# Expert stages of a two-layer network: where the counts become integers, and where the one-hots of the fetched pairs are built

## The chip, the cores and the metric

One NeuronCore of one Trainium2 chip runs the whole program. The metric is the device time of one execution, in microseconds (us). Five engines work side by side: TensorE (PE; its weight loads are PEld), VectorE (DVE), ScalarE (ACT), GpSimd (POOL) and SyncE (SP), which issues the weight transfers.

## The reference, cut to what matters

A sequence of 256 tokens of width 1024 passes through two blocks of two layers. Each of the two layers of the first block ends in a mixture of experts, and the change is in that part alone:

```python
scores = sigmoid(t @ router_w); sel = scores + router_b
best_group = argmax(sum of the two best of sel in each of 4 groups)
top_idx = the two best experts of that group;  top_w = their scores / sum
for e in range(16):
    he = silu(t @ w_gate[e]) * (t @ w_up[e])          # 1024 -> 512
    y = y + combine[:, e:e+1] * (he @ w_down[e])      # 512 -> 1024
```

Each token goes to two experts of one group of four. The 16 experts' weights are 96 MiB in each layer, and all of them are read.

## The kernel before

`moe(l)` runs twice, once for each layer of the first block. The experts go in eight pairs, p = 0 to 7. Each pair has 64 places for each of its two experts; a token beyond them goes through conditional blocks. The stage goes in this order:

- Router: `logits`, `scored`, ranks on VectorE, then `pick` (chosen or not) and `rk` (each token's place in its expert), `cnt` (the larger count of each pair) and `cs` (the weights).
- `hot` and `gather` bring the tokens of pairs 0 and 1 (`FIRST = 2`) to their places: a product with a one-hot gives `ph` in PSUM, and ScalarE writes it, scaled, to `hg`. `gather(0, 4)` stands ahead of the first pair's products and `gather(4, 8)` in the middle of its gate product.
- `tokens_of` builds one-hots (`ohb`, 12 operations of VectorE, L1393) for pairs 2 to 7; `indices` turns them into token numbers (`px`, `number`, `idx`). By these numbers GpSimd fetches those pairs' rows from a copy in DRAM (`rows`).
- `up(p)`: 32 products for the gate (`pg`) and 32 for the up weights (`pu`), all at L1482, then `hd`, and its transpose `hidT`. `down(p)`: 32 products `po` (L1531), scaled (`of`), split in two (`eo`); the scatter back into `x` (`py`) is held over into the next pair.
- Weights come by SyncE's queue in transfers of 1 MiB, 12 for a pair, into a ring of 17 slots, in order of use; a slot is filled again when the products that read it are done.

For pairs 2 to 7 there are conditional blocks. Every engine that takes part has to load the count into a register:

```python
count = nc.values_load(cnti[0:1, p:p + 1], min_val=0, max_val=S, engines=engines)  # L1669
with tc.If(count > 64):                                                            # L1671
    Sm, ws = more_up(p, W, hidT)
own = up(p, W, (lambda: rest(p, p - 5)) if p in (5, 6) else None)
with tc.If(count > 64):                                                            # L1674
    more_down(W, hidT, Sm, ws)
```

`rest`, at p = 5 and 6, does the same with the largest count (L1616, block at L1618). `cnti` is made by one conversion (L1341) of all eight counts to integers.

The order of each engine's instructions is not that of the text: a planner picks it from a modelled timeline, from what is ready. `pin(...)` sets an instruction behind the one that stands before it in the text on the same engine. The products at L1482 and L1531 are pinned, and so are the products of `gather` and the differences `xl` (L1273); in the kernel before the one-hots `ohb`, the conversion and the register loads are not.

Of the kernel before, what the change touches and what calls it, by code (L numbers as in the profile page):

```python
# [14 lines left out]
I32 = mybir.dt.int32  # L15
AF = mybir.ActivationFunctionType
ALU = mybir.AluOpType
# [4 lines left out]
P = 128  # L22
D = 1024
S = 256
# [9 lines left out]
FIRST = 2  # L34
# [86 lines left out]
class Net:  # L121
# [1107 lines left out]
    def moe(self, l):  # L1229
        nc, I, tc = self.nc, self.I, self.tc  # L1230
        V = nc.vector
        mm = nc.tensor.matmul
        A, B = self.scale_shift(l, 1)
        with self.phase(f"moe{l}", MOE_RING, True) as mp:
# [3 lines left out]
            pin = tc.keep_in_program_order  # L1238
            rbias = self.rbias
            gate = self.gate[l, 5]  # L1240
            slots = self.k("slots")
# [93 lines left out]
            cnt = mp.tile([1, 8], F32, name="cnt")  # L1335
# [1 line left out]

            V.tensor_scalar(cnt[:, 0:FIRST], cnt[:, 0:FIRST], 32.0, None, op0=ALU.add)
            V.tensor_reduce(cnt[:, 0:1], cnt, axis=AX.X, op=ALU.max)
            cnti = mp.tile([1, 8], I32, name="cnti")  # L1340
            V.tensor_copy(cnti, cnt)  # L1341


            cs = mp.tile([P, 2, 16], F32, name="cs")
# [42 lines left out]
            def tokens_of():  # L1387
                for h in range(2):
                    for t in range(2):
                        o = self.sp.tile([P, 3, 256], BF16, tag=("e2", "gt")[h], name="ohb")  # L1390
                        e = rk[:, t, 4 + 6 * h:10 + 6 * h].rearrange("p (q j) -> p q j", j=2).unsqueeze(3)
                        for c, n, s0 in ((0, 64, 0), (128, 32, 64), (192, 32, 64)):
                            V.tensor_tensor(o[:, :, c:c + 2 * n].rearrange("p q (j s) -> p q j s", j=2),  # L1393
                                            e.to_broadcast([P, 3, 2, n]),
                                            slots[:, s0:s0 + n].unsqueeze(1).unsqueeze(1).to_broadcast([P, 3, 2, n]),
                                            op=ALU.is_equal)
                        ones_of.append(o)

            def indices():
# [67 lines left out]
            def up(p, W, between=None):  # L1467

                if p == 0:
                    oneh.extend(hot((0, 1), 0, 64))  # L1470
                    parts(1, True)
                    gather(0, 4)
                    tokens_of()
                q = slice(128 * (p % 2), 128 * (p % 2) + 128)
                pg = self.bank([P, 512], name="pg")
                pu = self.bank([P, 512], name="pu")
                for w, pp in ((W[0], pg), (W[1], pu)):
                    for k in range(KD):
                        if p == 0 and w is W[0] and k == 4:
                            gather(4, 8)  # L1480
                        for j in range(2):
                            pin(mm(pp[64 * j:64 * j + 64, :], hg[0][:, p % 2, k, 64 * j:64 * j + 64], w[j][k // 4][:, k % 4, :],  # L1482
                                   start=k == 0, stop=k == KD - 1, tile_position=(0, 64 * j)))
                if between:
                    between()
                if p == 0:
                    self.split(cs, ch, cl)
                    indices()
                hd = self.sp.tile([P, 512], F32, tag="e1", name="hd")
                nc.scalar.activation(hd, pg, AF.Silu)  # L1490
                V.tensor_tensor(hd, hd, pu, op=ALU.mult)  # L1491

                if self.pending:
                    self.pending(2)
                hidT = self.sp.tile([P, 4, P], F32, tag="e2", name="hidT")
                turn_hidden(hd, hidT)
                if self.pending:
                    self.pending(2)
                Sm, ws = places([oneh[t][:, q] for t in range(2)], p) if p < FIRST else own_places.pop(0)
                if 1 <= p < 7:  # L1500
                    columns(got[0][:, (p + 1) % 2, 0:D], P, hg[0][:, (p + 1) % 2])
                    own_places.append(known(p + 1, 0, kept[:, p % 2, :]))
                    if p < 6:
                        rows(1, p + 2)
                    if p < 5:
                        rows(0, p + 3)
                return hidT, Sm, ws
# [91 lines left out]
            engines = (mybir.EngineType.PE, mybir.EngineType.DVE, mybir.EngineType.Activation)  # L1599
# [13 lines left out]
            def rest(p, t):  # L1613


                left = nc.values_load(cnti[0:1, 0:1], min_val=0, max_val=2 * S,  # L1616
                                      engines=engines + (mybir.EngineType.Pool,))
                with tc.If(left > 96):  # L1618
                    wv = mp.tile([P, 16], F32, tag="wv", name="wv")
                    space = [e.rearrange("p a d -> p (a d)")[:, 0:2048] for e in got]  # L1620
                    hc = hg[0][:, (p + 1) % 2]
                    hid = self.sp.tile([P, 4, P], F32, tag="e1", name="hide")
                    banks = [self.bank([P, 512], name="be") for i in range(6)]
                    V.tensor_scalar(wv[:, 0:2 * FIRST], rk[:, t, 0:2 * FIRST], 64.0, None, op0=ALU.is_gt)
                    V.tensor_scalar(wv[:, 2 * FIRST:], rk[:, t, 2 * FIRST:], 96.0, None, op0=ALU.is_gt)
                    V.tensor_tensor(wv, wv, cs[:, t, :], op=ALU.mult)
                    nc.gpsimd.dma_start(space[0][:, 0:D], xd[128 * t:128 * t + 128, 0:D])
                    columns(space[0][:, 0:D], P, hc, banks[0:2])
                    n = 0

                    def fetched(src, nd):
                        nonlocal n
                        n += 1
                        return self.fetch(space[n % 2].rearrange("p (k n) -> p k n", n=nd), src, "(p k) n -> p k n", nc.gpsimd)
                    for e in range(NE):
                        for i, src in enumerate(("exp_w_gate", "exp_w_up")):
                            for b in range(2):
                                w = fetched(I[src][l, e][512 * b:512 * b + 512, :], 512)
                                for k in range(4):
                                    mm(banks[2 + i], hc[:, 4 * b + k, :], w[:, k, :], start=b + k == 0, stop=b + k == 4)  # L1640
                        hd = self.sp.tile([P, 512], F32, tag="gt", name="hde")
                        nc.scalar.activation(hd, banks[2], AF.Silu)
                        V.tensor_tensor(hd, hd, banks[3], op=ALU.mult)
                        turn_hidden(hd, hid, banks[0])
                        for b in range(2):
                            w = fetched(I["exp_w_down"][l, e][256 * b:256 * b + 256, :], D)
                            for k in range(2):
                                for c in range(2):
                                    mm(banks[4 + c], hid[:, 2 * b + k, :], w[:, k, 512 * c:512 * c + 512], start=b + k == 0,
                                       stop=b + k == 2)  # L1650
                        for c in range(2):
                            sl = slice(512 * c, 512 * c + 512)
                            of = self.sp.tile([P, 512], F32, tag="gt", name="ofe")
                            V.scalar_tensor_tensor(of, banks[4 + c], wv[:, e:e + 1], gate[:, sl], op0=ALU.mult, op1=ALU.mult)
                            V.tensor_tensor(self.x[:, t, sl], self.x[:, t, sl], of, op=ALU.add)
                    for i, q in ((0, p + 1), (1, p + 1), (0, p + 2)):
                        if q < 8:
                            rows(i, q)

            for p in range(8):  # L1660
                W = first_two(p) + [weights("exp_w_down", 256, p)]
                if p == 7:
                    self.turn, self.nload = [self.ring] * RING, 0
                    self.resume()
                if p < FIRST:
                    down(W, *up(p, W))
                    continue

                count = nc.values_load(cnti[0:1, p:p + 1], min_val=0, max_val=S, engines=engines)  # L1669
                hidT = self.sp.tile([P, 4, 64], F32, tag="e2", name="hidTb")  # L1670
                with tc.If(count > 64):  # L1671
                    Sm, ws = more_up(p, W, hidT)
# [3 lines that stand above are left out]
                down(W, *own, p == 7)  # L1676
# [789 lines left out]
```

## Time and profile before

| | |
|---|---|
| median of 3 runs | 1591.37 us (1589.22 to 1593.0) |
| profiled execution, its own time | 1589.33 us |
| span of its trace | 1587.5 us |
| TensorE busy | 1481.6 us, 93% of the span |
| VectorE busy | 916.3 us, 58% |
| ScalarE busy | 673.7 us, 42% |
| granted TensorE clock, mean | 0.979 of full speed |
| DMA | 418.14 MB, mean 263 GB/s |

The trace shows about 1.8 us less than the execution's own time, which lie around the span. Busy TensorE time is modelled for the ends of the matmuls, so start to start tells more than the durations. The first expert stage begins at about 200 us with its router and ends at about 451 us; the second begins at about 598 us and ends at about 846 us.

### The profile page before, as it was taken

What the parts mean: (1) busy time and instruction counts of PE and PEld (TensorE: products, weight loads), DVE (VectorE), ACT (ScalarE), POOL (GpSimd) and SP (SyncE); (2) the same over time, 40 slices, a digit from 0 to 9 for tenths busy, and PEclk for the clock granted to TensorE, in tenths of its full rate; (3) what the DMA queues carried; (4) which work ended last, traced back from release to release, by engine and by line L of the source; (5) the groups of instructions that cost most, each with busy time, mean ns of one, the idle gap of its engine ahead of it and who ended that gap; (6) DMA issues with size and microseconds to landing.
All of it is one profiled execution on the core that took longest, in us unless ns stands there. A gap on an engine that the chain in (4) does not pass through costs nothing. (4 is left out here: it accounts for less than half of the span.)

```text
span 1587.5 us, 22950 instructions
## 1 busy us (share of the span) xinstructions
PE 1481.6 (93%) x8719; PEld 1043.2 (66%) x8719; DVE 916.3 (58%) x1788; ACT 673.7 (42%) x1404; POOL 141.3 (9%) x192
## 2 busy tenths in 40 slices
PE   6999969998989997999888999899999999999998
PEld 3666634334369973444335887788887997788886
DVE  4755543233269974223226776866667777766665
ACT  3434331111146543111105455665556666665554
POOL 0320001000000000100002100110001211110000
PEclk9999989999989998999999999999999999999999
DMA  9998979999967986999997541646554542546540
GB/s 357 350 314 298 355 310 419 418 418 417 412 212 249 318 322 271 419 418 417 418 417 248 149 134 67 198 161 206 192 171 152 176 144 81 190 155 205 193 159 27
DMA packets 172511, 418.14 MB, mean 263 GB/s; under 512 B 10376, under 2 KB 94016, under 8 KB 147792
## 3 DMA queue, kind: packets, MB, share of 16 engines
q1 hardware_dynamic: 165696, 403.46, 68.7%
q0 software_dynamic: 6400, 12.78, 2.4%
q8 instruction: 89, 1.46, 0.4%
q14 instruction: 54, 0.44, 0.1%
q10 hardware_dynamic: 272, 0.00, 0.0%
HBM read 422.13 MB, written 3.19 MB: 268 GB/s over the span
## 5 line engine op out<-in xcount | busy, mean ns | idle before, releaser
L230 DVE TENSOR_TENSOR hl<-w,hl 128x1024 fp32r<-128x1024 f32 x280 | 336.4, 1234 | 52.9 <-ACT hl L229 52.8
L229 ACT CAST hl<-w 128x1024 fp32r<-128x1024 f32 x280 | 280.2, 1045 | 33.5 <-DMA w<-in_even_w_in 20.5
L2341 PE MATMUL pgu<-hT,hl 128*128 128x512 f32 x640 | 224.3, 394 | 0.0
L2342 PE MATMUL pgu<-hT,hl 128*128 128x256 f32 x640 | 177.1, 277 | 0.0
L381 PE MATMUL lin<-hl,hThi 128*128 128x256 f32 (+2 forms) x480 | 159.4, 335 | 1.4 <-ACT hl L229 0.8
L382 PE MATMUL lin<-hl,hThi 128*128 128x256 f32 (+2 forms) x480 | 153.9, 321 | 2.0 <-DVE hl L230 1.9
L383 PE MATMUL lin<-hl,hTlo 128*128 128x256 f32 (+2 forms) x480 | 152.8, 320 | 0.0
L1482 PE MATMUL pg<-w,hg 128*64 128x512 f32 x512 | 120.1, 616 | 20.7 <-issue 17.0
L2341 PEld LDWEIGHTS pgu<-hT,hl 128*128 128x128 f32 x640 | 119.9, 187 | 27.8
L1491 DVE TENSOR_TENSOR hd<-hd,pu 128x512 f32<-128x512 f32 x16 | 11.0, 688 | 196.9 <-PE pu L1482 196.9
L1482 PE MATMUL pu<-w,hg 128*64 128x512 f32 x512 | 116.4, 593 | 6.0 <-DMA w<-in_exp_w_up 4.9
L2342 PEld LDWEIGHTS pgu<-hT,hl 128*128 128x128 f32 x640 | 120.2, 188 | 2.0
L1531 PE MATMUL po<-w,hidT 128*64 128x512 f32 x512 | 114.4, 599 | 6.0 <-PEq L1674 3.1
L381 PEld LDWEIGHTS lin<-hl,hThi 128*128 128x128 f32 x480 | 92.9, 194 | 16.8 <-issue 8.1
L1482 PEld LDWEIGHTS pg<-w,hg 128*64 128x64 f32 x512 | 41.6, 141 | 94.6 <-issue 78.8
L382 PEld LDWEIGHTS lin<-hl,hThi 128*128 128x128 f32 x480 | 93.0, 194 | 11.2 <-DVE hl L230 3.8
L383 PEld LDWEIGHTS lin<-hl,hTlo 128*128 128x128 f32 x480 | 92.7, 193 | 7.0 <-DVE hl L230 0.8
L1482 PEld LDWEIGHTS pu<-w,hg 128*64 128x64 f32 x512 | 41.4, 137 | 77.4 <-issue 67.0
L1531 PEld LDWEIGHTS po<-w,hidT 128*64 128x64 f32 x512 | 37.5, 138 | 72.8 <-issue 63.8
L1546 ACT CAST eo<-of 128x512 fp32r<-128x512 f32 x32 | 19.8, 617 | 132.4 <-DVE of L1543 132.2
L381 PE MATMUL linc<-hThi,hl 128*128 128x256 f32 x224 | 66.2, 296 | 0.0
L1438 ACT ACTIVATE hg<-hgT,ab 128x128 f32<-128x128 f32 x48 | 18.1, 457 | 110.3 <-PE hgT L184 110.2
(571 smaller groups left out, 2856.2 us busy)
## 6 DMA issues: line engine op xcount, KB each, us to landing
w<-in_exp_w_gate SPq DMA_DIRECT2D x64, 1024.0 KB, 17.8
w<-in_exp_w_down SPq DMA_DIRECT2D x64, 1024.0 KB, 19.8
w<-in_exp_w_up SPq DMA_DIRECT2D x64, 1024.0 KB, 17.3
w<-in_ada_w SPq DMA_DIRECT2D x48, 1024.0 KB, 7.2
w<-in_ffn_wg SPq DMA_DIRECT2D x22, 1024.0 KB, 5.5
w<-in_ffn_wu SPq DMA_DIRECT2D x22, 1024.0 KB, 7.5
w<-in_ffn_wd SPq DMA_DIRECT2D x22, 1024.0 KB, 8.9
w<-in_even_w_in SPq DMA_DIRECT2D x14, 1024.0 KB, 10.5
```

Source lines behind the costliest of these rows:

```text
L229: pin(self.nc.scalar.copy(w[:, 0], src))
L230: pin(self.nc.vector.tensor_tensor(w[:, 1], src, w[:, 0].bitcast(F32), op=ALU.subtract))
L381: pin(mm(out, lh, rh, start=start, stop=False))
L382: pin(mm(out, lh, rl, start=False, stop=False))
L383: pin(mm(out, ll, rh, start=False, stop=stop))
L1438: nc.scalar.activation(out[:, k, :], pt[:, k, :], AF.Identity, scale=self.ab[:, 0, b, k:k + 1], bias=self.ab[:, 1, b, k:k + 1])
L1482: pin(mm(pp[64 * j:64 * j + 64, :], hg[0][:, p % 2, k, 64 * j:64 * j + 64], w[j][k // 4][:, k % 4, :], start=k == 0, stop=k == KD - 1, til ...
L1491: V.tensor_tensor(hd, hd, pu, op=ALU.mult)
L1531: pin(mm(po[c][64 * j:64 * j + 64, :], hidT[:, k, 64 * j:64 * j + 64], W[2][j][k // 2][:, k % 2, 512 * c:512 * c + 512], start=k == 0, sto ...
L1546: nc.scalar.copy(eh[c], of)
L2341: mm(pp[i], wh[:, k, :], both[:, :, k, :], start=k == 0, stop=False)
L2342: mm(pp[i][:, 0, :], wl[:, k, :], hi[:, k, :], start=False, stop=k == KD - 1)
```

## The change

Three edits, all in `moe`. The one conversion of all counts becomes seven of one element each, each into a tile of its own: the count of pair p + 1 is converted behind the products `pg` and `pu` of pair p (for p = 1 to 6), that of `rest` behind those of pair 3, each pinned on VectorE. The register loads read those tiles. `tokens_of` moves from ahead of the first pair's products to behind them and behind the split of `cs`, and its operations are pinned.

```diff
             V.tensor_scalar(cnt[:, 0:FIRST], cnt[:, 0:FIRST], 32.0, None, op0=ALU.add)
             V.tensor_reduce(cnt[:, 0:1], cnt, axis=AX.X, op=ALU.max)
-            cnti = mp.tile([1, 8], I32, name="cnti")
-            V.tensor_copy(cnti, cnt)
+            number_of = {}
+
+            def count_of(*who):
+
+                for i in who:
+                    number_of[i] = mp.tile([1, 1], I32, name=f"cnti{i}")
+                    pin(V.tensor_copy(number_of[i], cnt[:, i:i + 1]))
...
                         for c, n, s0 in ((0, 64, 0), (128, 32, 64), (192, 32, 64)):
-                            V.tensor_tensor(o[:, :, c:c + 2 * n].rearrange("p q (j s) -> p q j s", j=2),
...
+                            pin(V.tensor_tensor(o[:, :, c:c + 2 * n].rearrange("p q (j s) -> p q j s", j=2),
...
                     gather(0, 4)
-                    tokens_of()
...
+                if FIRST <= p + 1 < 8:
+                    count_of(p + 1)
+                if p == 3:
+                    count_of(0)
                 if between:
                     between()
                 if p == 0:
                     self.split(cs, ch, cl)
+                    tokens_of()
                     indices()
...
-                left = nc.values_load(cnti[0:1, 0:1], min_val=0, max_val=2 * S,
+                left = nc.values_load(number_of[0][0:1, 0:1], min_val=0, max_val=2 * S,
...
-                count = nc.values_load(cnti[0:1, p:p + 1], min_val=0, max_val=S, engines=engines)
+                count = nc.values_load(number_of[p][0:1, 0:1], min_val=0, max_val=S, engines=engines)
```

## Rows read from the trace of the kernel before

**Rows 1.** The page's chart: DMA busy in tenths, 40 slices of 39.7 us.

```profile
DMA  9998979999967986999997541646554542546540
```

**Rows 2.** Timeline of PE, first stage: start, duration, line, out<-in, count, idle before.

```profile
213.04 0.28 PE L1375 MATMUL ph<-kept,xl 128*128 128x256 f32 x1
222.55 5.72 PE L1482 MATMUL pg<-w,hg 128*64 128x512 f32 x16 [9.23 <-issue]
228.19 0.39 PE L1375 MATMUL ph<-kept,xh 128*128 128x256 f32 x1
...
230.28 3.65 PE L1482 MATMUL pg<-w,hg 128*64 128x512 f32 x16
233.77 7.04 PE L1482 MATMUL pu<-w,hg 128*64 128x512 f32 x32
240.74 0.75 PE L1405 MATMUL px<-tok,ohb 128*128 128x1 bf16 x24
```

**Rows 3.** Timeline of PE, second stage, at the same place.

```profile
612.23 0.38 PE L1375 MATMUL ph<-kept,xl 128*128 128x256 f32 x1
620.41 6.46 PE L1482 MATMUL pg<-w,hg 128*64 128x512 f32 x16 [7.79 <-issue]
626.80 0.39 PE L1375 MATMUL ph<-kept,xh 128*128 128x256 f32 x1
```

**Rows 4.** Tile cnti: line, engine, operation, duration ns min/median/max, first and last start.

```profile
L1669 PEldq TENSOR_LOAD <-cnti x12: 294/299/487, 216.8 to 619.6; - x12
...
L1616 PEldq TENSOR_LOAD <-cnti x4: 305/308/309, 219.7 to 618.9; - x4
...
L1341 DVE CAST cnti<-cnt x2: 152/152/153, 216.6 to 614.6; 1x8 int32<-1x8 f32 x2
```

**Rows 5.** Timeline of DVE, first stage.

```profile
210.44 2.01 DVE L1273 TENSOR_TENSOR xl<-xn,xh 128x512 fp32r<-128x512 f32 x2
212.38 2.82 DVE L1393 TENSOR_TENSOR ohb<-rk,kt 128x384 bf16<-128x384 f32 x8
...
215.20 0.17 DVE L1349 TENSOR_TENSOR cs<-cs,den 128x32 f32<-128x32 f32 x1
...
216.57 0.15 DVE L1341 CAST cnti<-cnt 1x8 int32<-1x8 f32 x1
```

**Rows 6.** Timeline of ACT, first stage.

```profile
215.40 0.22 ACT L203 CAST ch<-cs 128x32 fp32r<-128x32 f32 x1 [6.99 <-DVE cs L1349]
215.54 1.93 ACT L1379 ACTIVATE hg<-ph,ab 128x256 f32<-128x256 f32 x4
```

**Rows 7.** Windows of the first stage: busy by engine, PEclk, DMA share, GB/s.

```profile
218.00:220.00 2.00, 0.00 (x0) 0.00 (x0) 0.00 (x0) 0.00 (x0) 0.00 (x0) 0.50 0.90 371
220.00:222.00 2.00, 0.00 (x0) 0.00 (x0) 0.00 (x0) 0.00 (x0) 0.00 (x0) 0.50 0.21 88
...
228.00:230.00 2.00, 2.00 (x17) 1.81 (x16) 0.00 (x0) 0.56 (x2) 0.00 (x0) 1.00 0.40 74
```

**Rows 8.** Windows of the second stage.

```profile
614.00:616.00 2.00, 0.00 (x0) 0.00 (x0) 0.82 (x5) 1.48 (x4) 0.42 (x1) 0.97 0.67 277
```

**Rows 9.** Line L1618, the branch around `rest` on PE.

```profile
L1618 PEldq COMPARE_BRANCH  x4: 5888/5960/6163, 380.4 to 795.9; - x4
```

**Rows 10.** Timeline of PE around the first branch of `rest`.

```profile
377.81 7.07 PE L1482 MATMUL pu<-w,hg 128*64 128x512 f32 x32
386.69 0.48 PE L1518 MATMUL py<-eo,kept 128*128 128x512 f32 x1 [1.81 <-PEq L1618]
```

**Rows 11.** The page's costliest groups: busy, mean ns, idle before, its releaser.

```profile
L1482 PE MATMUL pu<-w,hg 128*64 128x512 f32 x512 | 116.4, 593 | 6.0 <-DMA w<-in_exp_w_up 4.9
```

**Rows 12.** Timeline of PE, second stage, pair 5: the first such wait.

```profile
759.38 3.65 PE L1482 MATMUL pu<-w,hg 128*64 128x512 f32 x16 [1.30 <-DMA w<-in_exp_w_up]
```

**Rows 13.** Timeline of DVE: the last operation of down(0), during pair 1's products.

```profile
252.19 0.69 DVE L1547 TENSOR_TENSOR eo<-of,eo 128x512 fp32r<-128x512 f32 x1 [0.68 <-ACT eo L1546]
```

**Rows 14.** Timeline of PE: pair 1's first products.

```profile
250.14 7.04 PE L1482 MATMUL pg<-w,hg 128*64 128x512 f32 x32
```

More of the change, by code (lines that the diff above doesn't have):

```diff
@@ L1392, in tokens_of @@
                         for c, n, s0 in ((0, 64, 0), (128, 32, 64), (192, 32, 64)):
-                            V.tensor_tensor(o[:, :, c:c + 2 * n].rearrange("p q (j s) -> p q j s", j=2),
-                                            e.to_broadcast([P, 3, 2, n]),
-                                            slots[:, s0:s0 + n].unsqueeze(1).unsqueeze(1).to_broadcast([P, 3, 2, n]),
-                                            op=ALU.is_equal)
+                            pin(V.tensor_tensor(o[:, :, c:c + 2 * n].rearrange("p q (j s) -> p q j s", j=2),
+                                                e.to_broadcast([P, 3, 2, n]),
+                                                slots[:, s0:s0 + n].unsqueeze(1).unsqueeze(1).to_broadcast([P, 3, 2, n]),
+                                                op=ALU.is_equal))
                         ones_of.append(o)
```

## The prediction

> **What bounds the kernel now.** I read the chart first. DMA is at nine tenths from the seventh to the eleventh and from the 17th to the 21st slice, the two expert stages, and lower just before each [rows 1]. That looks like a kernel bound by weights; the timeline of TensorE says otherwise. All waits of the `pu` products for up weights come to 4.9 us in 16 pairs [rows 11], and the first stands in pair 5 of the second stage [rows 12]. In the first stage TensorE works from its first pair to its last nearly without a stop, so the end of that stage is set by when TensorE begins, and by what stops it on the way.
>
> So the beginning is the place to look. In the first stage the last product of `gather(0, 4)` starts at 213.04 and ends at about 213.32, and the first gate product starts at 222.55, 9.23 us later, with no releaser named ("issue") [rows 2]. In the second stage the same gap is 7.79 us, from 612.61 to 620.41 [rows 3]. What ends it? The gate product needs `hg`. ScalarE writes its first four parts from 215.54 on, in 1.93 us [rows 6], so all are there at 217.5, and PE still does not start for 5 us. What fills these 5 us are register loads: PE's loads of all the counts, six at L1669 and two at L1616 in each stage, begin at 216.8 [rows 4], right when the conversion is done (216.57 + 0.15 = 216.72 [rows 5]), and eight of them until 222.55 make 5.8 / 8 = 0.72 us each, of which 0.3 is the load itself. The planner has put them ahead of the first pair. This is the stall the change can take away.
>
> [...] And DMA runs dry: all 17 slots are full, its share falls to 0.21 in the window from 220, and comes back in the one from 228 [rows 7], when the first slots are read out.
>
> **The change, part by part.** *Conversions.* Seven of one element take the place of one of eight: at 0.15 us each [rows 4] one more microsecond of VectorE in a stage, spread over pairs 1 to 6. There VectorE waits for PE for most of each pair's products, so I count nothing; without that cover it would be 0.9 us in a stage. The gain lies in the data they carry: no load can now come before its conversion, and the first conversion is pinned behind the last operation of `down(0)`, which runs from 252.19 [rows 13], in pair 1. All eight loads leave the gap.
>
> *One-hots.* Eight of the 12 operations stand on VectorE between `xl` (until 212.45) and the normalizing of `cs` at 215.20 [rows 5], and `ch`, which ScalarE does ahead of `hg`, waits for `cs` [rows 6]. Pinned behind the split of `cs`, they leave this chain: `cs` can run at 212.45, that is 2.75 us sooner, `ch` and `hg` with it. So `hg` begins at 215.54 - 2.75 = 212.8, and its first part is there at about 213.4 (1.93 / 4 = 0.48 apart, the first a little longer). The 12 one-hots take 12 x 2.82 / 8 = 4.2 us [rows 5] and would run from about 213 to 217. Who needs them? `px`, at 240.74 now [rows 2], some 229 then: 12 us of cover. Were it gone, `px` and the row fetches behind it on GpSimd's queue would be late next.
>
> *Queues.* The write of `cs` to DRAM (GpSimd) goes out 2.75 us sooner; the three first row fetches move with the products. SyncE's weight transfers keep their order and go out when slots come free, sooner by what PE gains.
>
> *What PE then does, first stage.* It starts at 213.4 instead of 222.55. The 16 products took 228.19 - 222.55 = 5.64 us to the next one's start, mostly at the lower clock; at the full clock the same 16 take 233.77 - 230.28 = 3.49 us [rows 2]. PE has then been idle for hardly 0.1 us, and the lower clock stood in the rows only deep in the long gap, so I take 3.49. The second half of the gather starts at 213.4 + 3.49 = 216.9, not 228.19: **11.3 us**. The first slots come free at 216.9, while DMA still has work (share 0.90 from 218 to 220 [rows 7]), so its gap closes, about 9 us (by the shares of these windows, 220.2 to 229.2). If the stage had no slack in its weights, DMA's 9 us would be the limit and not 11.3: that is the lower bound of this term, and I take the upper one, since PE hardly waits for weights in this stage.
>
> *Second stage.* The DVE and ACT rows repeat there, 2.0 us earlier against PE's first products (four `hg` parts from 613.55). Moved up by 2.75 they are early enough for PE to go on right behind the gather, at 612.61: 612.61 + 3.49 = 616.1 against 626.80 [rows 3]: **10.7 us**. DMA's share is 0.67 in the window from 614 [rows 8], so it runs dry about when the first slots come free, and its own gain is as long as PE's.
>
> Together 22.0 us a run, if the loads cost nothing where they go.
>
> *The loads' new places.* The trace of before does not show a load amid products. Bounds: nothing, or all of 0.72 us. For nothing speaks the branch around `rest`: on PE it takes 5.96 us from 380.4 [rows 9], and the idle time it leaves is 1.81 us [rows 10], because the products ahead of it ran on until 384.9. PE's sequencer is thus some 4.5 us ahead of the array, and a load of 0.72 us fits in. For the full price speaks that the load must wait for its conversion: if the planner puts it where the conversion has just ended, the sequencer stands there, the lead is used up, and the array waits 0.72 us. Between these ends I take half: 8 x 0.36 = 2.9 us in the first stage (0 to 5.8). In the second, lost time is made up at the waits for up weights, 4.9 us [rows 11], which are DMA's and not PE's: 0 to 0.9, I take 0.4.
>
> [...]
>
> Sum: 11.3 + 10.7 - 2.9 - 0.4 = 18.7 us. Against the profiled execution's 1589.33: 1570.6. That execution lies 2.0 us below the median of the runs (1591.37), so the median of the changed kernel should be 1572.7. Less than 0.2% (3 us) can't be told from no change here.
>
> **The rivals.** *Loads at full price and more* (faster, by less): each load also waits about half a microsecond for its conversion. Then 8 x 1.2 = 9.6 in the first stage and 9.6 - 4.9 = 4.7 in the second: 22.0 - 14.3 = 7.7 us, 1583.7. For it: the planner did put these loads as early as it could. Against: the lead of 4.5 us.
>
> *Something else ready takes the loads' place.* `px` depends on the one-hots alone and is not pinned; put ahead of the gate products it makes PE wait until 217.2, and 0.75 for itself, and the clock is down again. Per stage 4.5 + 2.2 us of the gain are lost: 22.0 - 13.4 - 3.3 = 5.3, 1586; with the loads at full price it is a change of less than 3 us. Against: in the kernel before `px` was ready by 217 too and stayed behind the products [rows 2].
>
> *Slower.* A load put at the head of a pair's products, for a conversion pinned on VectorE behind work that ends late. In pair 1 that work ends at 252.88 [rows 13], and the products start at 250.14 [rows 14]: with conversion and load PE would stand until 253.8, 3.6 us. Eight such are 29 us in the first stage and 29 - 4.9 = 24 in the second: 53 - 22 = 31 us slower, 1622. It decides from 1.4 us a load in the first stage (11.3 / 8) and 1.95 in the second (15.6 / 8). Against: a planner that goes by what is ready would issue products there.
>
> *The lower clock anyway.* [...] On the rows, 16 products at the lower clock cost 2.2 us more in the first stage and 2.9 in the second: 18.7 - 5.1 = 13.6 us, 1577.7.
>
> **How the numbers follow.** The forecast (loads from free to 0.72, full clock) 0.57; lower clock 0.10; loads at full price and more 0.15; another instruction in their place 0.10; slower 0.05; the rest, some 0.03, no gain for a reason I don't see. Faster takes the first three and most of the fourth: 0.88; same 0.07; slower 0.05. The range goes from all of 22.0 with 3 us of scatter (1566) to the loads' rival with 2 us (1586).
>
> **What would show it.** In the profile after: no register load of PE between `gather(0, 4)` and the first gate product, which starts within 1 us of the gather's end; `ohb` behind `cl` on VectorE; granted clock 1.00 through the first pair; no dry stretch of DMA at either stage's start; and some 11 us less from `gather(0, 4)` to `gather(4, 8)` in each stage. Wrong if the idle time comes back amid pairs 1 to 6 at L1482 or L1669, or if PE waits for weights in pairs 5 and 6 by more than the 4.9 us of now, or if the next part of the kernel has to wait for its own weights and gives the time back.

## The result, and the profile after

The changed kernel takes 1570.58 us (median of 4 runs, 1568.27 to 1572.58) against 1590.46 of the kernel before on the same chip: 19.9 us less, a ratio of 0.9873 with a 95% interval of 0.9853 to 0.9892. The span of the profiled execution went from 1587.5 to 1567.2 us, by 20.3. The forecast was 18.7 us and 1572.7.

Where it came from is seen in the timeline of TensorE in the changed kernel, first and second stage (columns: start, duration, engine, line, operation, count, idle time before):

```profile
210.56 0.41 PE L1380 MATMUL ph<-kept,xh 128*128 128x256 f32 x1
...
213.54 0.28 PE L1380 MATMUL ph<-kept,xl 128*128 128x256 f32 x1
214.19 3.65 PE L1486 MATMUL pg<-w,hg 128*64 128x512 f32 x16 [0.37 <-ACT hg L1384]
217.77 0.39 PE L1380 MATMUL ph<-kept,xh 128*128 128x256 f32 x1
...
219.87 3.65 PE L1486 MATMUL pg<-w,hg 128*64 128x512 f32 x16
223.35 7.04 PE L1486 MATMUL pu<-w,hg 128*64 128x512 f32 x32
...
246.59 7.04 PE L1486 MATMUL pu<-w,hg 128*64 128x512 f32 x32
253.56 0.51 PE L1527 MATMUL py<-eo,kept 128*128 128x512 f32 x1
...
257.74 7.09 PE L1540 MATMUL po<-w,hidT 128*64 128x512 f32 x32
...
601.88 0.37 PE L1380 MATMUL ph<-kept,xl 128*128 128x256 f32 x1
602.18 3.65 PE L1486 MATMUL pg<-w,hg 128*64 128x512 f32 x16
605.76 0.39 PE L1380 MATMUL ph<-kept,xh 128*128 128x256 f32 x1
```

The gap of 9.23 us ahead of the first product [rows 2] is 0.37 us long, and what ends it is `hg`, a cause the profile can name. In the second stage [rows 3] there is none. The 16 products take 217.77 - 214.19 = 3.58 us where they took 5.64. `pu` of the first pair starts at 223.35 instead of 233.77. The stage itself began 0.47 us later in this execution (first `ph` at 210.56 instead of 210.09), so the gain there is 10.9 us.

The granted clock (the column before DMA's share) is 1.00 through the first stage's start, and DMA's share does not fall (0.93 to 1.05 from 210 to 226); in the second stage the clock is at 0.50 in the window before the products start, and DMA has a short dip from 604 to 608 (shares of 0.52 and 0.59):

```profile
214.00:216.00 2.00, 1.81 (x10) 0.67 (x12) 2.00 (x8) 1.51 (x4) 0.14 (x1) 1.00 1.04 430
...
218.00:220.00 2.00, 2.00 (x18) 1.86 (x19) 0.09 (x1) 0.97 (x3) 0.00 (x0) 1.00 1.04 439
...
600.00:602.00 2.00, 2.00 (x11) 2.00 (x10) 1.72 (x8) 1.24 (x3) 0.75 (x1) 0.50 1.01 426
602.00:604.00 2.00, 2.00 (x12) 0.68 (x12) 2.00 (x7) 1.02 (x2) 0.00 (x0) 0.98 1.01 426
604.00:606.00 2.00, 2.00 (x12) 0.62 (x9) 0.74 (x3) 0.00 (x0) 0.00 (x0) 1.00 0.52 217
```

The rows of [rows 7] at the same place had 0.50 for the clock and 0.21 for DMA.

Now the loads. By tile, in the changed kernel (duration in ns min/median/max, first and last start):

```profile
L1346 DVE CAST cnti<-cnt x14: 131/142/143, 242.4 to 633.6; 1x1 int32<-1x1 f32 x14
...
L1678 PEldq TENSOR_LOAD <-cnti x12: 297/301/488, 250.0 to 643.5; - x12
...
L1625 PEldq TENSOR_LOAD <-cnti x4: 298/299/303, 253.0 to 642.8; - x4
```

They begin at 250.0, in pair 1, and the order of PE's instructions in that pair (read from the built program, not from the trace; the number is the place in PE's stream) puts six in a row between `py` and the transpose `hT`, two more ahead of `po`:

```
896 L1486 MATMUL pu<-w,hg 64x512 [waits DMAHW5_49,PE_49]
...
904 L1527 MATMUL py<-eo,kept 128x512 [waits PE_49]
905 L1528 MATMUL py<-eo,kept 128x512
906 L1678 TENSOR_LOAD cnti_2172 [waits DVE_49]
907 L1678 ISA x2
908 L1678 TENSOR_LOAD cnti_2402 [waits DVE_49]
...
916 L1678 TENSOR_LOAD cnti_3181 [waits DVE_49]
917 L1678 ISA x2
918 L184 MATMUL hT<-kt,hd 128x128 [waits DVE_49]
```

Eight loads are some 5.8 us of the sequencer; from `pu` to `po` of pair 1 PE takes 257.74 - 246.59 = 11.15 us, and before it took the same 11.15 without any load there (257.00 to 268.15). They are free. The six in a row take 6 x 0.72 = 4.3 us from 250.0 on, and PE works on without a pause, past the transpose `hT` at 254.60; of the other two, the last in the second stage starts at 643.5, and there too PE works without a pause until `po` starts at 645.73.

On VectorE the one-hots now stand behind `cl` and delay nobody, and all seven conversions, the first here, run in pair 1, not pair by pair:

```profile
212.93 0.17 DVE L1354 TENSOR_TENSOR cs<-cs,den 128x32 f32<-128x32 f32 x1
213.39 0.19 DVE L204 TENSOR_TENSOR cl<-cs,ch 128x32 fp32r<-128x32 f32 x1 [0.28 <-ACT ch L203]
213.50 4.11 DVE L1398 TENSOR_TENSOR ohb<-rk,kt 128x384 bf16<-128x384 f32 x12
...
241.78 0.69 DVE L1556 TENSOR_TENSOR eo<-of,eo 128x512 fp32r<-128x512 f32 x1 [0.68 <-ACT eo L1555]
242.38 0.14 DVE L1346 CAST cnti<-cnt 1x1 int32<-1x1 f32 x1
```

In the order of VectorE's instructions each later conversion stands behind VectorE's own load of the count before, which the planner had also pulled forward; the pin held it to that load, not to the pair's work.

### The profile page after: what moved, and what is told of

Same layout as the page of the kernel before. It is cut to its first block, busy times and chain, and to the rows that moved or that the text cites. A ratio compares the mean times of both kernels' runs of the same rounds, so it can differ in the third digit from the quotient of the medians.

```text
span 1567.2 us, 22966 instructions
## 1 busy us (share of the span) xinstructions
PE 1477.5 (94%) x8719; PEld 1044.1 (67%) x8719; DVE 918.1 (59%) x1800; ACT 674.0 (43%) x1404; POOL 141.4 (9%) x192
## 5 line engine op out<-in xcount | busy, mean ns | idle before, releaser
L229 ACT CAST hl<-w 128x1024 fp32r<-128x1024 f32 x280 | 280.3, 1045 | 33.0 <-DMA w<-in_even_w_in 19.9
L1486 PE MATMUL pg<-w,hg 128*64 128x512 f32 x512 | 114.5, 595 | 4.1 <-PEq L1680 3.3
L382 PEld LDWEIGHTS lin<-hl,hThi 128*128 128x128 f32 x480 | 92.9, 194 | 10.9 <-DVE hl L230 3.5
```

The costliest lines, as they stand in the source:

```text
L229: pin(self.nc.scalar.copy(w[:, 0], src))
L382: pin(mm(out, lh, rl, start=False, stop=False))
```

## Experiments

### The two parts alone

*Conversions alone* (`counts_only`): the changed kernel with the one-hots at their old place.

```diff
                     gather(0, 4)
+                    tokens_of()                # and no pin in it
...
                     self.split(cs, ch, cl)
-                    tokens_of()
```

> The conversions as in the changed kernel, the one-hots of the fetched pairs back at their old place and unpinned. If both parts count, each for what it keeps back (the loads until 222.5 in the first stage, cs and with it hg for 2.75 us), the loads are out of the gap, but hg comes 2.7 us later than in the changed kernel: the first product starts some 2.5 us later in each stage, 5 us in all, so about 1575.5 with before at 1590.5. Rival, the one-hots are beside the point: no difference from the changed kernel, 1570.6. Rival, the gap was the one-hots' and not the loads': no faster than before.

Measured: 1577.04 us against 1590.54, ratio 0.9913 (0.9896 to 0.9929): 13.5 us gained, 6.4 fewer than the whole change.

*One-hots alone* (`onehots_only`): the changed kernel with the one conversion, unpinned.

```diff
-            number_of = {}                     # and count_of with its calls
+            cnti = mp.tile([1, 8], I32, name="cnti")
+            V.tensor_copy(cnti, cnt)
```

> The one-hots as in the changed kernel, one conversion of all counts as before, so that the planner puts PE's register loads ahead of the first pair again. If each load holds PE up for 0.72 us, eight of them begin when the conversion is done, some 3.5 us sooner than before, and end 3.5 us sooner: the first product starts 5 to 6 us after the gather, and the granted clock may still fall in that time. 3.5 to 5.5 us gained in each stage, 7 to 11 in all: about 1581. Rival, the first product waits for hg and the loads only fill the time: as the changed kernel, 1570.6.

Measured: 1582.78 us, ratio 0.9952 (0.9935 to 0.9968): 7.8 us gained. PE's first products in the two kernels, in each of the two stages, conversions alone first:

```profile
216.71 5.35 PE L1487 MATMUL pg<-w,hg 128*64 128x512 f32 x16 [2.83 <-ACT hg L1384]
221.99 0.39 PE L1380 MATMUL ph<-kept,xh 128*128 128x256 f32 x1
...
606.39 5.35 PE L1487 MATMUL pg<-w,hg 128*64 128x512 f32 x16 [2.83 <-ACT hg L1384]
```

```profile
219.49 6.54 PE L1481 MATMUL pg<-w,hg 128*64 128x512 f32 x16 [5.22 <-issue]
...
612.95 6.08 PE L1481 MATMUL pg<-w,hg 128*64 128x512 f32 x16 [5.07 <-issue]
```

With the loads out of the way the gap is 2.83 us, and its releaser is `hg`, late by the one-hots; with the one-hots out of the way it is 5.2 us, without a releaser, though `hg` is there at 215.9 (ScalarE writes it from 213.95, in 1.93 us). Eight loads of 0.72 us that end at 219.49 would begin at 213.7, an estimate, where they began at 216.8 before. Neither part is beside the point, and the rivals that gave the gap to one of them alone fall. The two gains add up to 13.5 + 7.8 = 21.3, near the 19.9 of both; that they come so near is partly chance, because the waits overlap.

`counts_only` lost more than the 5 us expected of the later `hg`, for the clock's sake: its windows show it falling when PE was already at work again, and the 16 products take 221.99 - 216.71 = 5.28 us instead of 3.58:

```profile
216.00:218.00 2.00, 1.29 (x6) 0.48 (x8) 1.29 (x5) 2.00 (x5) 0.73 (x1) 0.97 1.02 430
218.00:220.00 2.00, 2.00 (x8) 0.56 (x6) 0.00 (x0) 0.03 (x1) 0.00 (x0) 0.50 0.89 373
220.00:222.00 2.00, 2.00 (x9) 0.42 (x5) 0.00 (x0) 0.00 (x0) 0.00 (x0) 0.68 0.13 53
```

### One conversion for all counts, pinned

`one_conversion` keeps a single conversion of eight counts, pinned behind the products of pair 1.

```diff
-                if FIRST <= p + 1 < 8:
-                    count_of(p + 1)
-                if p == 3:
-                    count_of(0)
+                if p == 1:
+                    pin(V.tensor_copy(cnti, cnt))
```

> As the changed kernel, but all eight counts are made integers by one conversion, pinned behind the products of pair 1. In the profile of the changed kernel all seven conversions and all eight loads of PE lie in pair 1 anyway. If what counts is only that no load can stand ahead of the first pair, the time is that of the changed kernel within 1 us (1570 to 1572). Rival, spreading them over pairs is what keeps the loads cheap: some 3 us a stage slower, 1576.

Measured: 1571.13 us, ratio 0.9872 (0.9856 to 0.9889), which can't be told from the changed kernel's 0.9873. PE's first products again stand right behind the gather, and its loads begin at 250.5:

```profile
214.64 3.65 PE L1480 MATMUL pg<-w,hg 128*64 128x512 f32 x16 [0.50 <-ACT hg L1378]
...
603.32 3.65 PE L1480 MATMUL pg<-w,hg 128*64 128x512 f32 x16
```

That the counts are converted one by one gives nothing here; that the conversion is behind the first pair gives all of that part.

### What a register load amid products costs

Three kernels add loads of PE whose values are not used. `loads4` and `loads12` have 4 and 12 of them between the gate and the up products of pair 1, of a count converted long before; `late_wait` has one ahead of pair 1's gate products, of a count converted behind `down(0)`.

```diff
                 for w, pp in ((W[0], pg), (W[1], pu)):
+                    if p == 1 and w is W[1]:
+                        for i in range(4):     # 12 in the other
+                            ...                # a load of more_n on PE, set behind PE's instruction before it
```

> The changed kernel with four more register loads of PE, of a count that has long been there, pinned between the gate and the up products of pair 1 (their values are not used). If PE's sequencer is some 4.5 us ahead of its array, four loads (2.9 us) leave no idle time ahead of the up products: time as the changed kernel. Rival, the array stands for every load: 2.9 us of idle time ahead of pu in each stage, some 5.8 us in all.

> The same with twelve loads, 8.6 us of PE's sequencer. If its lead is 4.5 us, the array stands 8.6 - 4.5 = 4.1 us ahead of the up products of pair 1 in each stage, about 8 us in all at most (in the second stage up to 4 us of it come back at the waits for weights). Rival, every load is paid in full: 8.6 us a stage. Rival, loads are free whatever their number: no idle time.

```diff
+                if p == 1:
+                    late = mp.tile([1, 1], I32, name="late")
+                    pin(V.tensor_copy(late, cnt[:, 0:1]))
+                    ...                        # one load of late on PE, behind down(0)'s products
                 for w, pp in ((W[0], pg), (W[1], pu)):
```

> The changed kernel with one more register load of PE, pinned ahead of pair 1's gate products, of a count converted behind the last operation of down(0) on VectorE. That conversion ends some 2.8 us after pair 1's products start in the changed kernel. By the prediction's rival on the other side PE stands until the conversion and the load are done: 3.5 us in each stage for one load, 5 to 7 in all. If the lead hides it, nothing.

One run each: 1569.45, 1580.18 and 1581.46 us. The timeline of PE at the place, in `loads4`, `loads12` and `late_wait`:

```profile
240.54 7.04 PE L1495 MATMUL pg<-w,hg 128*64 128x512 f32 x32
247.41 7.04 PE L1495 MATMUL pu<-w,hg 128*64 128x512 f32 x32
```

```profile
240.99 7.04 PE L1495 MATMUL pg<-w,hg 128*64 128x512 f32 x32
252.17 10.09 PE L1495 MATMUL pu<-w,hg 128*64 128x512 f32 x32 [4.14 <-issue]
...
652.37 9.67 PE L1495 MATMUL pu<-w,hg 128*64 128x512 f32 x32 [4.04 <-issue]
```

```profile
245.66 8.78 PE L1494 MATMUL pg<-w,hg 128*64 128x512 f32 x32 [3.68 <-DVE cnti L1346]
...
641.33 7.09 PE L1494 MATMUL pg<-w,hg 128*64 128x512 f32 x32 [3.48 <-DVE cnti L1346]
```

Four loads cost nothing: `pu` starts 6.87 us after `pg`, as without them. Twelve are 12 x 0.72 = 8.6 us of the sequencer and leave 4.14 and 4.04 us of idle time: 4.5 us of them are hidden. That is the lead read from the branch around `rest` [rows 9, 10], found by another instruction at another place, and the rivals "paid in full" and "free whatever their number" both fall. The six loads that follow in the same pair still cost nothing there: from `pu` on, `loads12` has no idle time but what the changed kernel has. Its loss, 9.6 us in one run, is more than the 8 expected at most, and the clock has a part in it once more: `pu` takes 10.09 us instead of 7.04 (9.67 in the second stage), with 0.50 granted in the window:

```profile
252.00:254.00 2.00, 1.83 (x6) 0.69 (x8) 0.00 (x0) 0.00 (x0) 0.00 (x0) 0.50 1.00 416
```

`late_wait` shows the other half. One load, no longer than the others (0.31 and 0.49 us; those of the changed kernel take 0.30 to 0.49), stops PE for 3.68 and 3.48 us where the prediction's rival had 3.6, since what it waits for comes late (the conversion starts at 244.5, the load at 244.7); the lead of 4.5 us did not hide that. Its 10.9 us against the changed kernel, in one run, hold two things more: its first product starts at 216.28 instead of 214.19, 0.9 us of it in the gather, whose products took 0.41 us instead of 0.28, as in the changed kernel's second stage with 0.50 granted, and `pg` takes 8.78 us instead of 7.04 in the first stage, where the clock fell to 0.50 (0.73 from 246 to 248, 0.50 from 248 to 250). In the second stage, behind a pause of 3.48 us, `pg` took 7.09.

### A version that beats both

In the changed kernel two of the larger waits of PE that are left in the first stage stand in pair 5, at the conditional block `rest` (L1627) and at the block behind it (L1683). PE jumps over the 16 experts of `rest` in pair 5 and again in pair 6. The changed kernel's rows in pair 5:

```profile
376.32 0.47 PE L1527 MATMUL py<-eo,kept 128*128 128x512 f32 x1 [1.79 <-PEq L1627]
382.23 7.09 PE L1540 MATMUL po<-w,hidT 128*64 128x512 f32 x32 [2.39 <-PEq L1683]
```

`rest_once` does both halves of the tokens in one block, in pair 6.

```diff
-            def rest(p, t):
+            def rest(p):
...
                 with tc.If(left > 96):
+                    for t in range(2):         # around all but the tiles and the row fetches at the end
...
-                own = up(p, W, (lambda: rest(p, p - 5)) if p in (5, 6) else None)
+                own = up(p, W, (lambda: rest(p)) if p == 6 else None)
```

> The changed kernel with the block rest, which stands once in pair 5 and once in pair 6, put together into one block in pair 6 for both halves of the tokens. If the idle time of PE at the two branches of pair 5 (1.8 and 2.4 us in the first stage, 2.6 and some more in the second) comes from the long branch alone, it goes: 4 us in the first stage and up to 3 in the second, where PE waits for weights anyway; 1564 to 1567. Rival, a block of twice the length makes the branch of pair 6 as much longer: no difference, 1570.6.

Measured: 1562.02 us (5 runs, 1558.0 to 1566.31), ratio 0.9815 (0.9794 to 0.9836) to the kernel before: 29.3 us in all (the kernel before took 1591.35 in this series), 8.6 less than the changed kernel by the medians, more than expected. The branch that is left, on PE:

```profile
L1627 PEldq COMPARE_BRANCH  x2: 5984/6043/6102, 389.4 to 762.7; - x2
```

It takes 6.0 us, as long as each of the four did for half the block (5.9 us), so the rival of a longer branch falls. What it leaves idle is not the same everywhere: 1.02 us ahead of `pu` of pair 6 in the first stage, but 4.97 in the second, where the products behind it took 9.43 us instead of 7.05:

```profile
768.87 9.43 PE L1486 MATMUL pu<-w,hg 128*64 128x512 f32 x30 [4.97 <-PEq L1627]
```

From the stage's first `ph` to the last pair's `po` the first stage is 3.85 us shorter than in the changed kernel (430.80 - 211.65 against 433.56 - 210.56) and the second 2.6 (808.22 - 594.98 against 813.58 - 597.71), 6.5 in the two profiles; the remaining 2 us of the medians I can't place.

## Why the prediction was right

**Loads in the gap.** Right. [rows 4] gave the time, and `onehots_only`, where they remain, keeps a gap of 5.2 us with the same label "issue".

**One-hots ahead of `cs`.** Right, and the share was about as large as put: `counts_only` starts its products 2.5 us later than the changed kernel. `hg` begins at 213.57, the first product at 214.19; with the 0.47 us of a later start the forecast was 213.9. That 0.3 us, and 0.1 us of the 16 products (3.58 us for 3.49), is what the first stage lacks of the 11.3 (10.9 measured).

**Second stage.** 10.7 forecast; from the first `ph` to the last pair's `po` it is 215.87 us instead of 226.57, 10.7 shorter. The first stage is 10.8 shorter by the same marks. 21.5 in the stages, less 0.47 ahead of them and 0.7 behind them, makes the span's 20.3.

**The loads' price** was the term that was off: 3.3 us taken, 0 measured. The half between the bounds came from the thought that a load is put where its conversion has just ended; they ran 4 us after the last conversion (245.49 to 250.0), with the lead whole. `loads4` and `loads12` show the price as what goes beyond the lead of 4.5 us: nothing for 2.9 us of loads, 4.1 for 8.6. Without this term the sum was 22.0 us, against 21.5 measured in the two stages. That the forecast of 18.7 lies so near the 19.9 of the medians is in part luck: 3.3 us were taken off for nothing, and some 2 us went missing elsewhere (0.5 in the stages, 1.2 outside them, and 0.4 between the profiled spans and the medians).

**The clock.** Right for the changed kernel: 1.00 through the first pair of the first stage. In the second stage it is 0.50 in the window from 600, before the products start, and 0.98 in the window from 602, so the rival of the lower clock came close. It cost no more than before: the gather's products, 2.98 us from the first start to the last in the first stage, take 4.17 there, and 4.16 in the kernel before.

**DMA.** No dry stretch in the first stage; in the second a dip to 0.52 and 0.59 from 604 to 608, which the prediction had excluded. It cost nothing that shows: the wait of `pu` for up weights is 3.7 us now, less than the 4.9 of [rows 11]:

```profile
L1486 PE MATMUL pu<-w,hg 128*64 128x512 f32 x512 | 116.2, 593 | 4.6 <-DMA w<-in_exp_w_up 3.7 <-PEq L1627 1.0
```

**The conversions pair by pair** did not come about, and the prediction had them spread over pairs 1 to 6. It made no difference, as `one_conversion` shows. The rival on the slower side is one that `late_wait` shows, at about the price it was given (3.68 and 3.48 us for 3.6), and only its place was not taken by the planner.

## What to carry to other kernels

Look at an idle stretch with no releaser for what the engine's own sequencer does in it: register loads and branches are not counted as busy (here eight loads stood in 9.23 us of idle time). Such work belongs amid long products, up to the engine's lead over its array (4.5 us here: 2.9 us of loads left no idle time, 8.6 left 4.1), and its data must be ready well before (in `late_wait` they were not, and one load cost 3.7 us); a planner that goes by what is ready puts it into the first hole, which may be the start of a stage. To move it, hold back what it depends on, and check in the order of instructions where it went, since a pin only holds to the instruction that happens to stand before.

## What the runs showed of the hardware that was not expected

In these runs some pauses of PE cost more than their length, and the length alone did not decide it. After 2.83 us of idle time in `counts_only` the granted clock fell to 0.50 when the products were already running, and they took 1.7 us longer, in both stages. After 4.14 us in `loads12` they took 3.05 us longer, and after 4.97 us in the second stage of `rest_once` 2.4 us. After 3.68 us in the first stage of `late_wait` it was 1.7, but after 3.48 us in its second stage nothing. Ahead of `po` of pair 5, 2.39 us of idle time cost nothing more in the changed kernel, where the clock stayed at 1.00. And the branch around a block that is not taken cost PE's sequencer 5.9 us for 16 experts and 6.0 for twice as many.
